# Column units of a split-precision trunk: products in the order hi, hi, lo, lo instead of hi, lo, hi, lo

## The chip, the cores and the metric

The kernel runs on one core of a Trainium2 chip. Times are device microseconds of one execution; the time before is the median of three runs. A profiled execution shows every instruction of each engine: TensorE (PE, with its weight loads as PEld), VectorE (DVE), ScalarE (ACT), GpSimd (POOL) and SyncE (SP), which issues the weight transfers.

## The reference

Two layers of a streaming encoder over 256 tokens of width 2048, all in float32. Each layer normalises, projects, runs eight retention heads and eight blocks of a gated linear recurrence, joins both by an output projection, and ends with a SwiGLU feed-forward part of width 5632:

```python
for l in range(DEPTH):
    h = _rmsnorm(x, norm1_g[l])
    p = (h @ w_in[l]).astype(f32)
    q, k, v, g, xb, yb = jnp.split(p, [R, 2 * R, 3 * R, 4 * R, 4 * R + L], axis=-1)
    ...
    mix = jnp.concatenate([o_ret, o_lru], axis=-1).astype(x.dtype)
    x = x + mix @ w_out[l]
    h = _rmsnorm(x, norm2_g[l])
    x = x + (jax.nn.silu(h @ ffn_w_gate[l]) * (h @ ffn_w_up[l])) @ ffn_w_down[l]
return _rmsnorm(x, final_g)
```

## The kernel before

Activations lie transposed, features on the 128 partitions and the 256 tokens along the row. Every product with a weight matrix is made of float32r products (a reduced float32 that TensorE takes in one pass) of split operands: a high part, which is the value rounded to float32r, and a low part, which is the rest. High by high, high by low and low by high are added up; low by low is left out.

The work is a list of **units**, one for each 128 output features (`layer_units`, line 463). In each layer these are 8 units for v, 40 column units of w_in (with the heads' and the recurrences' work between them), 16 of w_out, and then, for each of three thirds of the feed-forward width (15, 15 and 14 blocks of 128), gate and up units in turn and 16 units of w_down. A unit's weights, up to 128 x 2048, come in one transfer three units ahead (`load`), and are split two units ahead by `split` (line 560) in two halves: ScalarE writes the high half `whi` (line 568), VectorE the low half `wlo` (line 569). Both have three buffers, so ScalarE's next writing waits for TensorE's last reading of a high buffer.

A **column unit** (`column_unit`, line 182) has one PSUM bank `acc_ps` of 512 columns. It goes over its tiles k (16, or 15 and 14 in w_down) in blocks of four; the instructions of heads and recurrences are put between blocks by a counter of ticks. Each tile makes two products. The first takes the tile's high weights against the operand's high and low parts side by side, 512 columns (line 196). The second takes the low weights against the operand's high part, 256 columns, and adds to the upper half of the bank (line 198). Each product has its own load of 128 x 128 weights. At the end ScalarE and VectorE (`joined_halves`, or `residual`) add the two halves.

The v units (lines 441 to 443) have it the other way round: the operand is loaded as weights and 512 columns of weights stream, three products for each tile and half of the tokens (high by high, high by low, low by high). Small products in plain float32 (lines 141 to 331) serve the norms, heads and gates: sums over partitions (141), spreading a row (157), and the heads' transposes (289), which read the normalised halves `on` that VectorE makes at line 275 from a power on GpSimd (line 268).

The program's order within an engine is the order of the code, moved a little by the tile scheduler.

Of the kernel before, what the change touches and what calls it, by code (L numbers as in the profile page):

```python
# [16 lines left out]
P = 128  # L17
T = 256
# [62 lines left out]
def trunk(ctx: ExitStack, tc, a, out):  # L81
# [12 lines left out]
    V, S, G, PE = nc.vector, nc.scalar, nc.gpsimd, nc.tensor  # L94
# [87 lines left out]
    def column_unit(src, n_k, operand, done, begin=None, order=None):  # L182

        u = Unit(src, n_k * P, [], begin=begin)
        order = order or list(range(n_k))

        def block(i):
            ks = order[i : i + 4]

            def run():  # L190
                if i == 0:
                    u.ps = big_ps.tile([P, 512], F32, tag="big", name="acc_ps")
                for k in ks:
                    w = slice(k * P, (k + 1) * P)
                    x2 = operand(k)
                    PE.matmul(u.ps, lhsT=u.hi[:, w], rhs=x2.rearrange("p a t -> p (a t)"),  # L196
                              start=k == order[0], stop=False)
                    PE.matmul(u.ps[:, T : 2 * T], lhsT=u.lo[:, w], rhs=x2[:, 0, :],  # L198
                              start=False, stop=k == order[-1])
            return run  # L200

        u.blocks += [block(i) for i in range(0, n_k, 4)]
        u.done = lambda: done(u.ps)
        return u
# [542 lines left out]
```

## Time and profile before

| | |
|---|---|
| median of 3 runs | 2271.38 us (2269.16 to 2271.72) |
| profiled execution, its own time | 2267.88 us |
| its span | 2266.1 us |
| TensorE | 2249.2 us busy, 99% of the span, 12760 products |
| weight loads | 1955.5 us, 86% |
| VectorE | 1514.8 us, 67% |
| ScalarE | 1127.0 us, 50% |
| GpSimd | 59.8 us, 3% |
| transfers | 422.92 MB, mean 187 GB/s |

The profile has a row for every instruction with its start and, for products, an end that is modelled. A product's record begins before the previous one's ends, so that durations of products add up to more than the time. Rows of the timeline give starts to 0.01 us; longer means come from counts in a stretch. The row of a load names the product that will use the weights.

### The profile page before, as it was taken

To read this page: it belongs to the slowest core of one execution; us is meant where nothing else is said; L and a number is where in the kernel's file an instruction comes from. 1 tells how busy PE (TensorE), PEld (TensorE's weight loads), DVE (VectorE), ACT (ScalarE), POOL (GpSimd) and SP (SyncE) were. 2 spreads that over 40 slices of the span, in tenths; PEclk is the share of its full clock that TensorE was granted. 3 is DMA by queue.
4 is the path that set the end of the run, shared out by engine and by line. 5 is a ranking of instruction groups with operands and counts; after the bars stand their busy time and mean duration, and the time that the engine had idled before them with its cause. 6 is when DMAs were issued, how large, how long until landed. Compare 5 with 4: busy or idle time off the path is not lost.

```text
span 2266.1 us, 31764 instructions
## 1 busy us (share of the span) xinstructions
PE 2249.2 (99%) x12760; PEld 1955.5 (86%) x12760; DVE 1514.8 (67%) x2405; ACT 1127.0 (50%) x1648; POOL 59.8 (3%) x97
## 2 busy tenths in 40 slices
PE   9999999999999999999999999999999999999997
PEld 7888888888888888888888888888888888888886
DVE  6888876666566665666748889766665566566665
ACT  6667544544344443444546665454443444334453
POOL 0010100000000000000000101000000000000000
PEclk9999999999999999999999999999999999999998
DMA  7555455555555555554555554555555555555553
GB/s 286 180 183 179 173 193 188 184 190 190 188 195 186 189 187 190 186 187 173 197 194 180 179 190 166 186 184 188 193 186 189 190 187 183 181 195 188 192 181 109
DMA packets 63141, 422.92 MB, mean 187 GB/s; under 512 B 7313, under 2 KB 7953, under 8 KB 24593
## 3 DMA queue, kind: packets, MB, share of 16 engines
q1 hardware_dynamic: 60912, 414.60, 52.2%
q0 software_dynamic: 1792, 5.24, 0.8%
q8 instruction: 100, 1.64, 0.3%
q10 hardware_dynamic: 288, 1.05, 0.1%
q14 instruction: 49, 0.39, 0.0%
HBM read 418.77 MB, written 2.10 MB: 186 GB/s over the span
## 4 chain that ended last, share of the span: by engine, by line
PE 97%; DVE 1%; issue 0%; DMA 0%; POOL 0%; ACT 0%; SPq 0%; DVEq 0%; POOLq 0%
PE acc_ps L196 61%; PE acc_ps L198 31%; PE v_ps L442 1%; PE v_ps L443 1%; PE v_ps L441 1%; PE sm_ps L331 1%; DVE wlo L569 0%; PE sm_ps L240 0%; DMA raw<-in_w_v_dram 0%; PE sm_ps L157 0%; DVE op L130 0%; PE sm_ps L289 0%; PE sm_ps L241 0%; PE sm_ps L255 0%; PE sm_ps L256 0%
## 5 line engine op out<-in xcount | busy, mean ns | idle before, releaser
L196 PE MATMUL acc_ps<-op,whi 128*128 128x512 f32 x6016 | 2117.0, 397 | 0.0
L198 PE MATMUL acc_ps<-op,wlo 128*128 128x256 f32 x6016 | 1681.1, 279 | 0.0
L196 PEld LDWEIGHTS acc_ps<-op,whi 128*128 128x128 f32 x6016 | 1129.1, 188 | 268.3 <-DVE op L127 1.7
L569 DVE TENSOR_TENSOR wlo<-raw,whi 128x1024 fp32r<-128x1024 f32 (+3 forms) x808 | 948.8, 1189 | 376.1 <-ACT whi L568 368.6
L568 ACT ACTIVATE whi<-raw 128x1024 fp32r<-128x1024 f32 (+3 forms) x808 | 817.1, 1029 | 665.0 <-PE acc_ps L196 587.3
L198 PEld LDWEIGHTS acc_ps<-op,wlo 128*128 128x128 f32 x6016 | 1134.2, 189 | 0.7
L406 DVE TENSOR_TENSOR x<-acc_ps,x 128x256 f32<-128x256 f32 x128 | 54.3, 424 | 216.6 <-PE acc_ps L198 216.6
L126 ACT ACTIVATE op<-mix 128x256 fp32r<-128x256 f32 x104 | 43.1, 416 | 172.3 <-DVE mix L510 163.7
L505 ACT ACTIVATE sg<-z 128x256 f32<-128x256 f32 x88 | 36.8, 418 | 161.2 <-DVE z L504 161.2
L179 DVE TENSOR_TENSOR z<-acc_ps,low 128x256 f32<-128x256 f32 x256 | 106.9, 418 | 0.0
L178 ACT ACTIVATE low<-acc_ps 128x256 f32<-128x256 f32 x256 | 93.7, 366 | 0.0
L127 DVE TENSOR_TENSOR op<-mix,op 128x256 fp32r<-128x256 f32 x104 | 43.9, 424 | 42.6 <-ACT op L126 42.6
L509 DVE TENSOR_TENSOR sg<-sg,rs 128x256 f32<-128x256 f32 x88 | 37.4, 425 | 42.6 <-ACT sg L505 42.6
L407 DVE TENSOR_TENSOR x<-acc_ps,x 128x256 f32<-128x256 f32 x128 | 54.4, 425 | 4.3
L150 POOL TENSOR_TENSOR rc<-rc,mhalf 128x2 f32<-128x2 f32 x7 | 5.8, 824 | 1727.9 <-DVE rc L149 1727.9
L442 PE MATMUL v_ps<-wlo,op 128*128 128x512 f32 x128 | 50.2, 392 | 1.2 <-DVE wlo L569 1.2
L441 PE MATMUL v_ps<-whi,op 128*128 128x512 f32 x128 | 49.9, 395 | 1.3 <-ACT op L129 1.3
L443 PE MATMUL v_ps<-whi,op 128*128 128x512 f32 x128 | 50.2, 392 | 0.0
L504 DVE TENSOR_TENSOR z<-z,rs 128x256 f32<-128x256 f32 x88 | 36.9, 419 | 0.0
L510 DVE TENSOR_TENSOR mix<-z,sg 128x256 f32<-128x256 f32 x88 | 36.9, 419 | 0.0
L129 ACT ACTIVATE op<-x,par 128x256 fp32r<-128x256 f32 x64 | 31.2, 496 | 1.1 <-DMA par<-in_par_dram 1.1
L173 DVE TENSOR_TENSOR acc<-acc,sq 128x256 f32<-128x256 f32 x73 | 30.6, 419 | 1.0 <-ACT sq L172 1.0
(116 smaller groups left out, 699.4 us busy)
## 6 DMA issues: line engine op xcount, KB each, us to landing
raw<-in_w_gate_dram SPq DMA_DIRECT2D x88, 1024.0 KB, 4.8
raw<-in_w_up_dram SPq DMA_DIRECT2D x88, 1024.0 KB, 4.8
raw<-in_w_in_dram SPq DMA_DIRECT2D x80, 1024.0 KB, 4.8
raw<-in_w_down_dram SPq DMA_DIRECT2D x64, 960.0 KB, 4.7
raw<-in_w_out_dram SPq DMA_DIRECT2D x32, 1024.0 KB, 4.8
raw<-in_w_down_dram SPq DMA_DIRECT2D x32, 896.0 KB, 4.6
raw<-in_w_v_dram SPq DMA_DIRECT2D x12, 1024.0 KB, 4.8
raw<-in_w_v_dram SPq DMA_DIRECT2D x16, 256.0 KB, 6.0
```

The lines of the kernel that those rows point to most:

```text
L127: V.tensor_tensor(out=t[:, 1, :], in0=x_ap, in1=t[:, 0, :].bitcast(F32), op=ALU.subtract)
L178: S.activation(out=low, in_=ps[:, T : 2 * T], func=AF.Copy)
L179: V.tensor_tensor(out=z, in0=ps[:, 0:T], in1=low, op=ALU.add)
L196: PE.matmul(u.ps, lhsT=u.hi[:, w], rhs=x2.rearrange("p a t -> p (a t)"), start=k == order[0], stop=False)
L198: PE.matmul(u.ps[:, T : 2 * T], lhsT=u.lo[:, w], rhs=x2[:, 0, :], start=False, stop=k == order[-1])
L406: V.tensor_tensor(out=X[:, k, :], in0=ps[:, T : 2 * T], in1=X[:, k, :], op=ALU.add)
L407: V.tensor_tensor(out=X[:, k, :], in0=ps[:, 0:T], in1=X[:, k, :], op=ALU.add)
L441: PE.matmul(ps, lhsT=x2[:, 0, t], rhs=u.hi[:, w], start=k == 0, stop=False)
L442: PE.matmul(ps, lhsT=x2[:, 0, t], rhs=u.lo[:, w], start=False, stop=False)
L443: PE.matmul(ps, lhsT=x2[:, 1, t], rhs=u.hi[:, w], start=False, stop=k == KD - 1)
L568: S.activation(out=u.hi[:, w], in_=u.raw[:, w], func=AF.Copy)
L569: V.tensor_tensor(out=u.lo[:, w], in0=u.raw[:, w], in1=u.hi[:, w].bitcast(F32), op=ALU.subtract)
```

## The change

Within each block of four tiles, the loop goes over pairs of tiles: both high products of the pair, then both low products. In a block of three the last tile stands alone (high, low). Sums are the same, in another order.

```diff
             def run():
                 if i == 0:
                     u.ps = big_ps.tile([P, 512], F32, tag="big", name="acc_ps")
-                for k in ks:
-                    w = slice(k * P, (k + 1) * P)
-                    x2 = operand(k)
-                    PE.matmul(u.ps, lhsT=u.hi[:, w], rhs=x2.rearrange("p a t -> p (a t)"),
-                              start=k == order[0], stop=False)
-                    PE.matmul(u.ps[:, T : 2 * T], lhsT=u.lo[:, w], rhs=x2[:, 0, :],
-                              start=False, stop=k == order[-1])
+                for pr in (ks[:2], ks[2:]):
+                    for k in pr:
+                        PE.matmul(u.ps, lhsT=u.hi[:, k * P : (k + 1) * P],
+                                  rhs=operand(k).rearrange("p a t -> p (a t)"), start=k == order[0], stop=False)
+                    for k in pr:
+                        PE.matmul(u.ps[:, T : 2 * T], lhsT=u.lo[:, k * P : (k + 1) * P], rhs=operand(k)[:, 0, :],
+                                  start=False, stop=k == order[-1])
             return run
```

TensorE, inside a column unit of w_in in layer 0, before (`op` is an operand's pair of parts, `whi` and `wlo` the unit's weights; the numbers tell buffers apart):

```order
L196 MATMUL acc_ps_887<-op_169,whi_774 128x512
L198 MATMUL acc_ps_887<-op_169,wlo_775 128x256
L196 MATMUL acc_ps_887<-op_182,whi_774 128x512
L198 MATMUL acc_ps_887<-op_182,wlo_775 128x256
L196 MATMUL acc_ps_887<-op_193,whi_774 128x512
L198 MATMUL acc_ps_887<-op_193,wlo_775 128x256
L196 MATMUL acc_ps_887<-op_206,whi_774 128x512
L198 MATMUL acc_ps_887<-op_206,wlo_775 128x256
```

The same four tiles after the change:

```order
L195 MATMUL acc_ps_887<-op_169,whi_774 128x512
L195 MATMUL acc_ps_887<-op_182,whi_774 128x512
L198 MATMUL acc_ps_887<-op_169,wlo_775 128x256
L198 MATMUL acc_ps_887<-op_182,wlo_775 128x256
L195 MATMUL acc_ps_887<-op_193,whi_774 128x512
L195 MATMUL acc_ps_887<-op_206,whi_774 128x512
L198 MATMUL acc_ps_887<-op_193,wlo_775 128x256
L198 MATMUL acc_ps_887<-op_206,wlo_775 128x256
```

The second tile's high product went ahead of the first tile's low one; high products are line 195 now.

TensorE, around the transposes of a late head in layer 0 (`on` is what they read, `sm_ps` what they write), before:

```order
L196 MATMUL acc_ps_2845<-op_169,whi_2684 128x512
L198 MATMUL acc_ps_2845<-op_169,wlo_2685 128x256
L196 MATMUL acc_ps_2845<-op_182,whi_2684 128x512
L289 MATMUL sm_ps_2854<-ident_85,on_2819 128x128
L198 MATMUL acc_ps_2845<-op_182,wlo_2685 128x256
L196 MATMUL acc_ps_2845<-op_193,whi_2684 128x512
L289 MATMUL sm_ps_2854<-ident_85,on_2819 128x128
L198 MATMUL acc_ps_2845<-op_193,wlo_2685 128x256
```

And after:

```order
L195 MATMUL acc_ps_2845<-op_169,whi_2684 128x512
L289 MATMUL sm_ps_2854<-ident_85,on_2819 128x128
L195 MATMUL acc_ps_2845<-op_182,whi_2684 128x512
L198 MATMUL acc_ps_2845<-op_169,wlo_2685 128x256
L198 MATMUL acc_ps_2845<-op_182,wlo_2685 128x256
L289 MATMUL sm_ps_2854<-ident_85,on_2819 128x128
L195 MATMUL acc_ps_2845<-op_193,whi_2684 128x512
```

The first transpose has two products fewer ahead of it, the second one fewer; it is the same in layer 1.

VectorE, at the same place (`on` are the two normalised halves, line 127 the low part of another operand), as a piece of the difference:

```order
 L569 TENSOR_TENSOR wlo_2768<-raw_2585,whi_2767 128x1024
+L275 TENSOR_SCALAR on_2819<-sm_ps_2750,mv_2786,ve_2791 128x128
 L127 TENSOR_TENSOR op_2804<-mix_2802,op_2804 128x256
-L275 TENSOR_SCALAR on_2819<-sm_ps_2750,mv_2786,ve_2791 128x128 x2
+L275 TENSOR_SCALAR on_2819<-sm_ps_2750,mv_2786,ve_2791 128x128
 L179 TENSOR_TENSOR z_2831<-acc_ps_2771,low_2830 128x256
```

The operand's subtraction stands between the two halves now, in layer 0 alone. Two more places differ on VectorE (a weight half ahead of one head's scores, and in the last w_down units of layer 0 the sum of squares between two weight halves) and two on ScalarE (a weight half between two operand copies); GpSimd and SyncE are as before.

## Rows read from the trace of the kernel before

**Rows 1.** The page: busy time by engine, and the chain by engine and line.

```profile
PE 2249.2 (99%) x12760; PEld 1955.5 (86%) x12760; DVE 1514.8 (67%) x2405; ACT 1127.0 (50%) x1648; POOL 59.8 (3%) x97
...
PE 97%; DVE 1%; issue 0%; DMA 0%; POOL 0%; ACT 0%; SPq 0%; DVEq 0%; POOLq 0%
PE acc_ps L196 61%; PE acc_ps L198 31%; PE v_ps L442 1%; PE v_ps L443 1%; PE v_ps L441 1%; PE sm_ps L331 1%; DVE wlo L569 0%; PE sm_ps L240 0%; DMA raw<-in_w_v_dram 0%; PE sm_ps L157 0%; DVE op L130 0%; PE sm_ps L289 0%; PE sm_ps L241 0%; PE sm_ps L255 0%; PE sm_ps L256 0%
```

**Rows 2.** The page's groups: line, tiles, count; busy us, mean ns; idle before.

```profile
L196 PE MATMUL acc_ps<-op,whi 128*128 128x512 f32 x6016 | 2117.0, 397 | 0.0
L198 PE MATMUL acc_ps<-op,wlo 128*128 128x256 f32 x6016 | 1681.1, 279 | 0.0
...
L173 DVE TENSOR_TENSOR acc<-acc,sq 128x256 f32<-128x256 f32 x73 | 30.6, 419 | 1.0 <-ACT sq L172 1.0
```

**Rows 3.** Timeline in w_down, layer 0: start us, duration us, instruction.

```profile
599.74 0.39 PE L196 MATMUL acc_ps<-op,whi 128*128 128x512 f32 x1
599.97 0.28 PE L198 MATMUL acc_ps<-op,wlo 128*128 128x256 f32 x1
599.97 0.19 PEld L196 LDWEIGHTS acc_ps<-op,whi 128*128 128x128 f32 x1
600.08 0.39 PE L196 MATMUL acc_ps<-op,whi 128*128 128x512 f32 x1
...
600.78 0.39 PE L196 MATMUL acc_ps<-op,whi 128*128 128x512 f32 x1
```

**Rows 4.** Timeline 300 us later, first and last of four high products.

```profile
899.75 0.40 PE L196 MATMUL acc_ps<-op,whi 128*128 128x512 f32 x1
...
900.81 0.40 PE L196 MATMUL acc_ps<-op,whi 128*128 128x512 f32 x1
```

**Rows 5.** Line 196 by stretch: length, PE (products), PEld (loads), PEclk; sums of five.

```profile
566.00:811.00 245.00, 245.00 (x708) 132.20 (x707) 1.00 0.54 191
...
sum 872.00, PE 872.00 PEld 471.39; mean PE 174.40 PEld 94.28
...
815.00:1054.00 239.00, 239.00 (x677) 127.05 (x677) 1.00 0.53 187
...
sum 729.00, PE 729.00 PEld 387.57; mean PE 145.80 PEld 77.51
```

**Rows 6.** The same view, two pieces of layer 0's projection, all of layer 1's.

```profile
99.50:117.50 18.00, 18.00 (x52) 9.58 (x51) 1.00 0.53 178
146.50:155.50 9.00, 9.00 (x27) 4.88 (x26) 1.00 0.54 194
1177.00:1430.00 253.00, 236.46 (x661) 123.92 (x660) 1.00 0.52 183
```

**Rows 7.** Timeline in the v units, the first and last of four products.

```profile
1150.03 0.39 PE L442 MATMUL v_ps<-wlo,op 128*128 128x512 f32 x1
...
1150.71 0.39 PE L442 MATMUL v_ps<-wlo,op 128*128 128x512 f32 x1
```

**Rows 8.** Timeline at 43.8 us: eight sums over partitions, merged, with their loads.

```profile
43.81 1.08 PEld L141 LDWEIGHTS sm_ps<-ones,sq 128*128 128x128 f32 x8
...
44.04 0.95 PE L141 MATMUL sm_ps<-ones,sq 128*128 128x1 f32 x8
44.82 0.19 PEld L441 LDWEIGHTS v_ps<-whi,op 128*128 128x128 f32 x1
```

**Rows 9.** Timeline at the last head's transposes in layer 0.

```profile
276.37 0.39 PE L196 MATMUL acc_ps<-op,whi 128*128 128x512 f32 x1
276.95 0.73 DVE L275 TENSOR_SCALAR on<-sm_ps,mv,ve 128x128 f32<-128x128 f32 x2 [0.62 <-POOL ve L268]
...
277.50 0.30 PE L289 MATMUL sm_ps<-ident,on 128*128 128x128 f32 x1 [0.74 <-DVE on L275]
...
277.99 0.27 PE L289 MATMUL sm_ps<-ident,on 128*128 128x128 f32 x1
```

**Rows 10.** Who waited for whom: us in total, times, longest us.

```profile
ACT whi L568 <- PE acc_ps L196: 587.3, 332, 4.0
...
PEld acc_ps L196 <- DVE op L127: 1.7, 6, 0.3
```

## The prediction

> **What bounds the kernel now.** Begin with the busy times and the chain of waits [rows 1]. TensorE is busy 99% of the span, and 97% of the chain that ended last lies on it: 61% on line 196 (the high parts), 31% on line 198 (the low parts). VectorE (67%), ScalarE (50%) and the transfers are cover; the time is set by how closely the 6016 pairs of products follow each other.
>
> The durations of the matmul records don't tell that: 397 and 279 ns [rows 2] overlap, since the next product starts before the record of the last one ends. Go by starts. In the timeline of a w_down stretch [rows 3] a high product starts at 599.74, its low product at 599.97, the next high one at 600.08; three pairs take 1.04 us. The load for that next high product starts at 599.97, together with the low product: each load runs under the product ahead of its own. At the granted 2.4 GHz (PEclk 1.00 in all stretches of [rows 5]) 512 columns take 213.3 ns and 256 take 106.7, 320 together; the spacing is some 26 ns above that.
>
> In another stretch the same instructions stand further apart [rows 4]: 899.75 to 900.81 is 1.06 us for three pairs. Busy time by stretch tells how long each spacing lasts [rows 5]: divide a stretch's length by its loads of line 196, one for each pair. Close: 245 us / 707 = 346.5 ns. Wide: 239 / 677 = 353.0 ns. Five long stretches are close (from 399, 566, 1520, 1941 and 2180 us on), 872 us together, so 2517 pairs; five are wide (from 309, 815, 1058, 1430 and 1686 on), 729 us, so 2065 pairs. The same piece of the program (w_down of the first third, then gate and up of the second) runs close from 566 in layer 0 and wide from 1686 in layer 1: the spacing belongs to no kind of unit. It changes where something interrupts the stream, and then stays. The input projections (660 loads in that of layer 1, as many in the other) are interrupted often and hold both spacings: 18 us / 51 = 352.9 in one piece and 9 / 26 = 346.2 in another [rows 6].
>
> **The change part by part.** Nothing is added or taken away: the same 12,032 products and loads, with the same columns. Two high products now follow each other, then two low ones; of 6016 tiles only 64 (the 15th of w_down's units with 15 tiles) stay high, low. Three effects:
>
> 1. *The spacing.* Before, every load of low weights ran under a high product and every load of high weights under a low one. Now, of four loads, two still run under high and two under low products; new is that high follows high and low follows low. High after high has a near row: in the v units products of 512 columns, each with a load of its own, start 0.68 us apart for three (1150.03 to 1150.71), 226.7 ns each [rows 7]. In the close spacing high to low takes 230 ns and low to high the rest, 116.5 [rows 3], so v's is 3.3 ns less. Low after low has no row. Its lower bound is the 106.7 ns of its columns. Its upper bound is the spacing of loads that nothing covers: eight loads with products of one column took 1.08 us, the last of them 0.19, so (1.08 - 0.19) / 7 = 127 ns each [rows 8]. I take 116.5, the nearest row, since there, too, a load must end under 256 columns. For high after high I take the 230 of this kind of unit and keep v's 226.7 for the range. Two tiles then cost 2 x 346.5 ns, the close spacing, and as the one uniform sequence that the trace has (v) keeps its spacing, I take it to last. Gain: 2065 pairs x 6.5 ns = 13.4 us, and in the projections half of some 1320 x 6.5 ns = 4.3 us (between 0 and 8.6). Together -17.7 us.
>
> 2. *The order around the transposes.* In each layer TensorE waits once for the last head's normalised halves: it does a high product at 276.37 and then nothing until 277.50, when the first transpose follows the half that VectorE began at 276.95; the second is at 277.99 [rows 9]. The new order has two products fewer ahead of the first transpose, 0.23 + 0.12 us that now stand behind the wait: +0.35 us a layer. VectorE puts an operand's subtraction (0.42 us) between the two halves in layer 0; three products instead of two now lie between the transposes and hide it, or else it is 0.4 us more. Two small spreads move up by one product of 0.12 us a layer, at a wait as well. Sum +0.9 us, between 0 and 1.3. ScalarE's moved copies and the moved sums in the last w_down third of layer 0 I cost at 0: two further units are already split. Without that cover a moved sum would be 0.42 us [rows 2] a unit, on 15 units 6 us.
>
> 3. *Releases and first uses.* A unit's last high product ends one low product (0.12 us) earlier, and ScalarE, which waited for it 332 times, 587.3 us in all [rows 10], may overwrite the buffer earlier. That wait isn't on the chain: worth 0. The last product of a unit stays a low one, so residuals and gates begin as before. In the second tile of a pair an operand is read 0.12 us earlier; TensorE's six waits for operands were 1.7 us [rows 10], so this is 0.7 us at most, and I take 0.
>
> Sum: -17.7 + 0.9 = -16.8 us on the profiled 2267.9 us, which gives 2251.1. The median of the runs shown is 2271.4, 3.5 us above the profiled one, so 2254.6 there.
>
> **Rivals.**
>
> *No change of the mean: both spacings remain.* For: what is counted under what is the same in both orders (two loads under long, two under short products for two tiles), and the spacings change after interruptions, which the change leaves in place. Some stretches then swap spacings; one of 700 pairs is worth 700 x 6.5 = 4.6 us. Time: 2272, within 9. Against: another rhythm need not have the old two spacings. The Trainium skill (TensorE: Matmul & The Clock Gate, "LDWEIGHTS (loading the stationary operand)") has a rule on this side: a load takes its columns over 1.2 GHz, 107 ns for 128, which is as long as 256 columns stream; by that every load just fits under either product, in either order, and the sum would be 0. The trace agrees only in part: low to high takes some 10 ns more than that.
>
> *Slower: two short products in a row can't cover two loads.* The place is the second low product of each pair of tiles. Its load begins only when the first low product does, and the next one's when it begins itself; before, a long product, in which a late stream catches up, came behind each short cover. If the gap there is the 127 ns of [rows 8] in place of 116.5, that is 10.5 ns x 3008 = +32 us on the close spacing, 2286. If the new rhythm settles in the wide spacing everywhere, it is 2517 x 6.5 = 16.4, 4.3 and 0.9 us above before: 2293. It decides from 17.7 us / 3008 = 5.9 ns per two tiles on; there the gain is eaten up. For: low to high is the gap in which a load has least cover. Against: 116.5 ns shows that a load does end under 256 columns.
>
> *Faster still.* With v's 226.7 ns from high to high it is 3.3 x 3008 = 10 us less, 2244.6, and with high to low at 226.7 as well 2235. Against: 3 ns may be only where a record begins.
>
> **How the numbers follow.** About 0.2% (4.5 us) is what a measurement of this kernel can tell from no change. The close spacing throughout, or better, has a chance of 0.42; both spacings 0.26 (0.07 faster, 0.13 the same, 0.06 slower); slower by the loads or the wide spacing 0.32. So faster 0.49, same 0.13, slower 0.38. The forecast is 2254.6, with a range of its own of 2242 to 2262. As cases of both signs count, the range is 2238 to 2296: it leaves out v's spacing in both gaps, and a 127 ns gap on top of the wide spacing.
>
> **What would show it.** In the timeline: high to high and high to low 0.23 us, low to low and low to high 0.12, two tiles in 0.693 us, and this in all ten long stretches, none at 0.706. Wrong would be a gap of 0.127 or more from low to low, or stretches that still differ. The transposes of the last head should wait some 0.35 us longer, and TensorE keep its 97% of the chain.

## The result and the profile after

The changed kernel takes 2257.81 us (median of 4 runs, 2257.48 to 2258.28) against 2271.35 us before (4 runs, 2269.16 to 2271.72): a ratio of 0.9938, with a 95% interval of 0.9926 to 0.9951, 13.5 us less. In a later comparison of 6 with 11 runs it was 2258.33 against 2272.65, 0.9930 (0.9917 to 0.9942). The profiled execution took 2257.48 us, 10.4 less than that of before.

The page after, busy times, chain and the two groups of products, to be held against [rows 1, 2]:

```profile
PE 2239.1 (99%) x12760; PEld 1949.4 (86%) x12760; DVE 1512.5 (67%) x2405; ACT 1127.1 (50%) x1648; POOL 59.8 (3%) x97
...
PE 97%; DVE 1%; issue 0%; DMA 0%; POOL 0%; ACT 0%; SPq 0%; DVEq 0%; POOLq 0%
...
L195 PE MATMUL acc_ps<-op,whi 128*128 128x512 f32 x6016 | 1899.8, 397 | 0.0
...
L198 PE MATMUL acc_ps<-op,wlo 128*128 128x256 f32 x6016 | 1188.6, 278 | 0.0
```

Nothing changed its part: TensorE has 97% of the chain, VectorE and ScalarE do as much as before. The busy sums of lines 195 and 198 fell by 217 and 493 us only because records of the same line that overlap now count once; the mean records, 397 and 278 ns, are those of before. So go by starts. The timeline after (`x2` is two instructions, the start is the first one's), at the place of [rows 3]:

```profile
600.02 0.39 PE L198 MATMUL acc_ps<-op,wlo 128*128 128x256 f32 x2
...
600.25 0.63 PE L195 MATMUL acc_ps<-op,whi 128*128 128x512 f32 x2
...
600.71 0.40 PE L198 MATMUL acc_ps<-op,wlo 128*128 128x256 f32 x2
...
600.94 0.40 PE L195 MATMUL acc_ps<-op,whi 128*128 128x512 f32 x1
```

Two low products take 0.23 us (600.02 to 600.25), two high ones 0.46 (to 600.71), together some 0.695 for two tiles. Line 195 by stretch (length; products; loads), to be held against [rows 5]:

```profile
566.00:808.00 242.00, 218.60 (x696) 106.30 (x695) 1.00 0.54 189
815.00:1045.00 230.00, 207.82 (x661) 100.98 (x660) 1.00 0.54 188
...
1679.00:1925.00 246.00, 222.25 (x707) 107.93 (x705) 1.00 0.54 190
```

242 / 695 = 348.2, 230 / 660 = 348.5 and 246 / 705 = 348.9 ns a tile (a load counted too many or too few is 0.5 ns). Before, the stretch from 815 was wide (353.0), that from 566 close (346.5) and that from 1686 wide. All three have one spacing now, 1.7 to 2 ns above the close one and nearly 5 below the wide one.

Where the time came from can be read off four markers, the sums over partitions at the end of w_out and of the feed-forward part in each layer. Before:

```profile
395.65 0.61 PE L141 MATMUL sm_ps<-ones,acc 128*128 128x1 f32 x4
1135.58 0.61 PE L141 MATMUL sm_ps<-ones,acc 128*128 128x1 f32 x4
1516.86 0.61 PE L141 MATMUL sm_ps<-ones,acc 128*128 128x1 f32 x4
2251.04 0.50 PE L529 MATMUL sm_ps<-ones,acc 128*128 128x1 f32 x4
```

After:

```profile
392.70 0.50 PE L141 MATMUL sm_ps<-ones,acc 128*128 128x1 f32 x4
1129.96 0.54 PE L141 MATMUL sm_ps<-ones,acc 128*128 128x1 f32 x4
1508.53 0.50 PE L141 MATMUL sm_ps<-ones,acc 128*128 128x1 f32 x4
2241.20 0.50 PE L529 MATMUL sm_ps<-ones,acc 128*128 128x1 f32 x4
```

The lead grows to 2.95, 5.62, 8.33 and 9.84 us: 2.95 in layer 0's projections, heads and w_out, 2.67 in its feed-forward part, 2.71 and 1.51 in layer 1. In the feed-forward parts, stretches that had been close cost a little more and the wide ones much less.

The wait at the last head's transposes after the change ([rows 9] show it before):

```profile
274.10 0.39 PE L195 MATMUL acc_ps<-op,whi 128*128 128x512 f32 x1
...
274.97 0.41 DVE L275 TENSOR_SCALAR on<-sm_ps,mv,ve 128x128 f32<-128x128 f32 x1 [0.92 <-POOL ve L268]
...
275.53 0.30 PE L289 MATMUL sm_ps<-ident,on 128*128 128x128 f32 x1 [1.04 <-DVE on L275]
...
276.14 0.28 PE L289 MATMUL sm_ps<-ident,on 128*128 128x128 f32 x1
```

From the start of the last high product to the first transpose it was 1.13 us (276.37 to 277.50) and is now 1.43: 0.30 more, at the place that the new order gave. In layer 1 the lead falls by 0.30 us at the same place.

### The profile page after: what moved, and what is told of

The parts are those of the page before. It is cut to its first block, busy times and chain, and to the rows that moved or that the text cites. A ratio compares the mean times of both kernels' runs of the same rounds, so it can differ in the third digit from the quotient of the medians.

```text
span 2255.7 us, 31764 instructions
## 1 busy us (share of the span) xinstructions
PE 2239.1 (99%) x12760; PEld 1949.4 (86%) x12760; DVE 1512.5 (67%) x2405; ACT 1127.1 (50%) x1648; POOL 59.8 (3%) x97
## 4 chain that ended last, share of the span: by engine, by line
PE 97%; DVE 1%; issue 0%; DMA 0%; POOL 0%; ACT 0%; SPq 0%; DVEq 0%; POOLq 0%
PE acc_ps L195 62%; PE acc_ps L198 31%; PE v_ps L442 1%; PE v_ps L443 1%; PE v_ps L441 1%; PE sm_ps L331 1%; DVE wlo L569 0%; PE sm_ps L240 0%; DMA raw<-in_w_v_dram 0%; DVE op L130 0%; PE sm_ps L289 0%; PE sm_ps L157 0%; PE sm_ps L241 0%; PE sm_ps L256 0%; PE sm_ps L255 0%
## 5 line engine op out<-in xcount | busy, mean ns | idle before, releaser
L195 PE MATMUL acc_ps<-op,whi 128*128 128x512 f32 x6016 | 1899.8, 397 | 0.0
L198 PE MATMUL acc_ps<-op,wlo 128*128 128x256 f32 x6016 | 1188.6, 278 | 0.0
L195 PEld LDWEIGHTS acc_ps<-op,whi 128*128 128x128 f32 x6016 | 920.4, 189 | 4.8 <-DVE op L127 0.7
L179 DVE TENSOR_TENSOR z<-acc_ps,low 128x256 f32<-128x256 f32 x256 | 106.7, 417 | 0.0
```

The source lines that it names most:

```text
L179: V.tensor_tensor(out=z, in0=ps[:, 0:T], in1=low, op=ALU.add)
L195: PE.matmul(u.ps, lhsT=u.hi[:, k * P : (k + 1) * P], rhs=operand(k).rearrange("p a t -> p (a t)"), start=k == order[0], stop=False)
L198: PE.matmul(u.ps[:, T : 2 * T], lhsT=u.lo[:, k * P : (k + 1) * P], rhs=operand(k)[:, 0, :], start=False, stop=k == order[-1])
```

## The experiments

**Is the spacing chosen by the place, or by chance?** First, the kernel before once more, without an edit (`before_2`).

> The kernel before, unchanged, profiled once more. If each interruption leaves the old order in one of two spacings by a chance of timing, other stretches than in the first profile are close and wide, and the time differs by the pairs that changed (6.67 ns each) within some 2263 to 2282. If the place decides, the same five stretches are close (from 399, 566, 1520, 1941 and 2180 us on).

It took 2275.07 us, 7.2 more than its first profile. Line 196 by stretch:

```profile
399.00:561.00 162.00, 162.00 (x460) 86.17 (x459) 1.00 0.51 181
570.00:815.00 245.00, 245.00 (x694) 130.25 (x694) 1.00 0.53 185
824.00:1062.00 238.00, 238.00 (x675) 126.63 (x674) 1.00 0.53 186
...
1695.00:1944.00 249.00, 249.00 (x706) 132.47 (x705) 1.00 0.53 187
1949.00:2183.00 234.00, 234.00 (x677) 126.22 (x676) 1.00 0.54 190
```

162 / 459 = 352.9 and 245 / 694 = 353.0: both stretches were close in the first profile (468 loads in the first, and 707 in 245 us). The same program, on the same instructions, was wide there. 1175 pairs by 6.5 ns are 7.6 us, near the difference of the two executions. So the place alone doesn't decide, and stretches that come out close or wide can explain why runs of the kernel before differ from each other: beside the groups of experiments below they lay between 2260.42 and 2281.71 us. But it isn't plain chance either. The other eight long stretches had the spacing of the first profile; three of them are shown (353.1, 353.2 and 346.2 ns). In the four profiles of the old order in these widths (`before`, `before_2`, and below `kick_before` and `lolow`) the stretches that begin at 309, 815, 1430 and 1686 in the first one are wide each time, and that from 1941 is close each time; the other five differ. What makes the choice stays open.

Then 37 small interruptions, one extra product of one column each, in either kernel (`kick_before`, `kick_after`):

```diff
     for n, u in enumerate(units):
+        if n >= 64 and n % 9 == 4:
+            PE.matmul(small()[:, 0:1], lhsT=ones, rhs=ones[:, 0:1], start=True, stop=True)
         if u.begin:
```

> The kernel before, with one extra product of a single column (float32, into a PSUM tile that nothing reads) ahead of every ninth unit from the 64th on, 37 in all. Theory 'two rhythms' (the old order has two spacings, 346.5 and 353.0 ns a tile, and an interruption decides which one follows): the long stretches break up, some pieces between two extra products run at 346.5 and some at 353.0; time 2271 plus 37 x 0.1 to 0.3 us, so 2275 to 2282, with a change of the mix worth up to 13 us either way. Rival 'place' (the spacing belongs to the place in the program, by its buffers or transfers): each piece keeps the spacing it had, close from 566 on and wide from 815 on.

> The changed kernel with the same 37 extra products. Theory 'one rhythm' (hi, hi, lo, lo has a single spacing, 348.3 ns a tile, to which every interruption returns): all pieces at 348.3, time 2257.8 plus 37 x 0.1 to 0.3 us, so 2262 to 2269. Rival 'chance' (the new order has two spacings as well, and the interruptions happened to leave it in the closer one): some pieces near 353, up to 2285.

Measured: 2282.98 us (2277.98 to 2286.37) and 2266.60 us (2266.23 to 2267.18). Line 196 between the extra products, old order:

```profile
412.00:459.00 47.00, 47.00 (x136) 25.32 (x136) 1.00 0.51 179
462.00:509.00 47.00, 47.00 (x137) 25.35 (x136) 1.00 0.50 181
...
610.00:656.00 46.00, 46.00 (x131) 24.43 (x130) 1.00 0.53 182
659.00:707.00 48.00, 48.00 (x137) 25.55 (x136) 1.00 0.51 177
...
761.00:809.00 48.00, 48.00 (x137) 25.52 (x136) 1.00 0.51 174
...
909.00:957.00 48.00, 48.00 (x137) 25.51 (x136) 1.00 0.51 177
```

136 loads need 47 us in the first pieces and 48 us in later ones, 346 and 353 ns; the wide pieces at 610 and 761 lie where the first profile was close. But the extra products didn't do this. 31 of the 37 stand outside the projections, in long stretches (that at 459.7 us between the first two pieces, that at 656.5 between the next two), and behind each of the 31 the spacing is the one ahead of it. From w_out on, in all four profiles of the old order, the spacing changes only at the start of a feed-forward part and near the end of the first unit of each w_down. There TensorE waits for an operand that has just been made (in units of 14 tiles the scheduler has also put two high products in a row there). In the first profile, at 564.26:

```profile
564.26 0.19 PEld L196 LDWEIGHTS acc_ps<-op,whi 128*128 128x128 f32 x1 [0.33 <-DVE op L127]
```

Line 195 in the new order:

```profile
409.00:456.00 47.00, 42.40 (x136) 20.41 (x135) 1.00 0.51 179
...
656.00:703.00 47.00, 42.40 (x136) 20.57 (x136) 1.00 0.52 181
...
903.00:949.00 46.00, 41.47 (x134) 20.09 (x132) 1.00 0.52 183
```

135 or 136 loads in 47 us and 132 in 46, and runs within 0.95 us, against 8.4 us in the old order. 'One rhythm' holds, 'chance' falls. As the extra products don't move the old order either, they say little by themselves; what bears it out is that the new order has the same spacing behind each wait for an operand, in this profile and in those of the changed kernel. The old order was wide in more places here than in the first profile, which can account for part of its 11.5 us over the kernel before beside it (2271.45).

The changed kernel in more runs, without an edit (`after_2`):

> The changed kernel, unchanged, in more runs. If its rhythm doesn't depend on what an execution leaves it in, all runs lie within 2256.5 to 2259.5 while those of the kernel before beside it spread over 10 us or more, and its profile has 348.3 ns a tile in all stretches. If the first runs were luck, some lie 4 us or more away. Against the version with whole units grouped (2257.14) it should be 0.5 to 1 us slower, if that difference is real.

2258.33 us (2257.55 to 2258.59); those of the kernel before beside it spread from 2270.71 to 2278.00, 7.3 us rather than 10. The spacing in its profile is 348.2 again (695 loads from 566 to 808), and near 348 in all ten long stretches.

**Is it the change of width that costs?** Groups of four and of eight tiles (`g4`, `g8`):

```diff
-                for pr in (ks[:2], ks[2:]):
+                for pr in (ks,):
```

> The changed kernel with groups of four: hi, hi, hi, hi, lo, lo, lo, lo in each block. Theory 'rhythm' (what matters is whether the pattern locks, the loads under long and short products being as many as before): 346.7 to 353.3 ns a tile, time 2247 to 2290, no gain that grows with the length of the group. Rival 'change of width' (the time above the streams of 320 ns is paid where the width changes): high after high nears the 226.7 ns of the v units and low after low 113, so 341.6 ns a tile or less, 40 us below the changed kernel, 2218.

For eight, blocks one and two (three and four) of a unit share their eight tiles: six high products, then two high and eight low.

> Groups of eight: of every eight tiles all high products, then all low ones. Rhythm: as with four, 2247 to 2290, and the gaps inside a run of high products still above 226.7 ns on average or the gaps inside a run of low ones at 120 (256 columns and the same 13.3 ns that a product of 512 columns has above its stream in the v units). Change of width: 340 ns a tile, 2208; high after high 226.7, low after low 113.

Measured: 2269.90 us (2268.95 to 2270.64) and 2264.94 us (2264.10 to 2265.31), both slower than pairs. High products by stretch, with four (line 195) and with eight (line 194):

```profile
570.00:815.00 245.00, 191.04 (x700) 119.25 (x700) 1.00 0.54 189
```

```profile
567.00:812.00 245.00, 175.83 (x702) 126.14 (x703) 1.00 0.54 189
```

350.0 ns and 348.5 to 349. Longer runs didn't come near the 341.6 or 340 ns of 'change of width'. Half the change (`g2mix`):

```diff
-                for pr in (ks[:2], ks[2:]):
+                for pr in (ks[:2], ks[2:3], ks[3:]):
```

> Blocks of four tiles as hi, hi, lo, lo, hi, lo, hi, lo: half of the change. Theory 'one rhythm for each pattern': a single spacing between 346.7 (13.3 ns for each product above its stream, the least seen) and 353.3, little spread between runs, time 2248 to 2288. Rival 'mean of the two': 348.3 in the grouped half and 346.5 or 353 in the alternating half, times that spread by some 5 us between runs.

2275.14 us (2274.93 to 2275.52): one rhythm, with the least spread of all, and a bad one. Line 195:

```profile
570.00:815.00 245.00, 232.44 (x698) 119.07 (x698) 1.00 0.53 188
```

351.0 ns, more than equal shares of the grouped order (348.2) and of the alternating one (350, the mean of close and wide) would make. With an alternating half that is always wide (353.0) equal shares would make 350.6, so the time alone doesn't tell a spacing of the pattern's own from a wide half that keeps. What is shown is that this pattern, too, varies little from run to run.

Whole units (`g16`): all high products of a unit, then all low ones, in blocks of 6 high, 6 high, 4 high and 4 low, 12 low (5384 of the 6016 tiles; w_out, the first gate unit and the first unit of each w_down stay in pairs):

```diff
+                if whole:
+                    j = i // 4
+                    steps = [((0, 6), (0, 0)), ((6, 12), (0, 0)), ((12, n_k), (0, 4)), ((0, 0), (4, n_k))][j]
...
+                for k in (range(*steps[0]) if whole else []):
...
+                for k in (range(*steps[1]) if whole else []):
```

> The changed kernel, but in w_in, gate, up and w_down units (not in w_out, nor in the first gate and first w_down units) all high products of a unit go ahead of all low ones. By 'two widths' with the 20 ns that a change from the runs of low to the runs of high took with eight, now once in 16 tiles: 346.7 + 20 / 16 = 347.9 ns a tile against 348.3, 2 us below the changed kernel, 2255 to 2258, if no operand is waited for longer; with later waits up to 2262. If the cost grows with the run (four: 350.3, eight: 349.2) rather than standing for a change: 348 to 350, 2258 to 2268.

2257.14 us (2256.45 to 2257.63; ratio to before 0.9947, 0.9930 to 0.9965). Three windows of its timeline, from 600, 601.9 and 604.2 us on, in a w_down unit of 15 tiles, give the number of products of each run that a window still holds, and the start of the first of them (line 200 high, 203 low):

```profile
600.14 3.59 PE L200 MATMUL acc_ps<-op,whi 128*128 128x512 f32 x15
603.57 1.96 PE L203 MATMUL acc_ps<-op,wlo 128*128 128x256 f32 x15
605.36 0.40 PE L200 MATMUL acc_ps<-op,whi 128*128 128x512 f32 x1
```

```profile
601.53 2.20 PE L200 MATMUL acc_ps<-op,whi 128*128 128x512 f32 x9
```

```profile
603.92 1.60 PE L203 MATMUL acc_ps<-op,wlo 128*128 128x256 f32 x12
```

The last nine high products take 603.57 - 601.53 = 2.04 us, 226.7 ns each, the value of the v units [rows 7]; the last twelve low ones 1.44 us, 120.0 each. So in a long run a product costs 13.3 ns more than its columns at 2.4 GHz (213.3 and 106.7 ns), at both widths. After the change from low to high the first six high products take 1.39 us, 231.7 each, 30 ns more in all; the first three low ones 0.35 us, 10 ns less than three of 120. A unit therefore pays 20 ns, and 5.22 us / 15 = 348.0 a tile. Two products at these long-run costs, 226.7 + 120.0 = 346.7, are the close spacing of the old order. No order tried here settled below this floor: the close stretches had nothing to gain, and only the wide ones could be won back.

**Is the load too long for its cover?** Low products of 128 columns (`lo128`; the low weights are left out for the last 128 tokens):

```diff
-                    PE.matmul(u.ps[:, T : 2 * T], lhsT=u.lo[:, w], rhs=x2[:, 0, :],
+                    PE.matmul(u.ps[:, T : T + 128], lhsT=u.lo[:, w], rhs=x2[:, 0, 0:128],
```

> The kernel before, hi and lo in turn, with low products of 128 columns in place of 256 (the low weights are left out for the last 128 tokens). Theory 'load' (under a low product the load of the next weights is what ends last, some 112 to 120 ns): low to high stays at 112 to 120 ns and a tile at 340 to 353, time 2230 to 2272 although 53 ns of streaming a tile are gone. Rival 'stream' (a product costs its columns and 13.3 ns, as 226.7 for 512 in the v units and 120 for 256 inside the runs of eight): low to high 67 ns, a tile 293, time about 1920.

2229.41 us (two runs): 53 ns less streaming a tile bring 43 us against the kernel before beside it (2272.41), not 320. (In the profiled run the granted clock fell to 1.2 GHz in four short pieces of the projections, 17 us together; the stretch read below has 2.4 GHz.) The timeline and line 196 by stretch:

```profile
600.14 0.22 PE L198 MATMUL acc_ps<-op,wlo 128*128 128x128 f32 x1
600.15 0.19 PEld L196 LDWEIGHTS acc_ps<-op,whi 128*128 128x128 f32 x1
600.20 0.44 PE L196 MATMUL acc_ps<-op,whi 128*128 128x512 f32 x1
600.25 0.19 PEld L198 LDWEIGHTS acc_ps<-op,wlo 128*128 128x128 f32 x1
600.48 0.22 PE L198 MATMUL acc_ps<-op,wlo 128*128 128x128 f32 x1
...
570.00:780.00 210.00, 210.00 (x619) 115.92 (x618) 1.00 0.55 195
```

A tile is 210 us / 618 = 339.8 ns, and 339.8 - 226.7 leaves 113 ns from low to high, far more than the low product's columns: the load. My forecast of the gap was wrong in its form. The high product's record begins 0.06 us after the low one, 0.05 after its own load began. In the other timelines a load starts together with the product ahead of its own; here the load of the next low weights starts at 600.25, so that is where the high product's stream began, 0.11 after 600.14. No run shows less than 226.7 ns for a high product, so a load takes 113 ns at most, 7 less than the 120 of a low product. It may be shorter: from the load of the high weights to the next load (600.15 to 600.25) it is 107.7 ns on the mean of 500 tiles from 600 to 770 us, and what is left of the tile, 232.3, is then a high product with some 6 ns of the extra that the wide spacing has as well. The Trainium skill (TensorE: Matmul & The Clock Gate, "LDWEIGHTS (loading the stationary operand)") gives a load its columns over 1.2 GHz, by which 128 columns would take 107 ns, an estimate that the run doesn't contradict. At 113 or less it fits under every gap of the other orders, of which the shortest, from low to low, are 113 to 115 ns; it sets the time here at 128 columns, and not at 320 or 512.

The other side, low products of 320 columns (`lo320`):

```diff
-                    PE.matmul(u.ps[:, T : 2 * T], lhsT=u.lo[:, w], rhs=x2[:, 0, :],
+                    PE.matmul(u.ps[:, 0:320], lhsT=u.lo[:, w], rhs=x2.rearrange("p a t -> p (a t)")[:, 0:320],
```

> The kernel before with low products of 320 columns (they go to the lower half of the bank and take in 64 tokens of the operand's low part; more is added up than before, nothing is left out). Theory 'load' (the old order has a wide spacing because the load of the high weights barely fits under 256 columns): with 26.7 ns more cover there is one spacing, the streams of 346.7 and twice 13.3 ns, 373.3 a tile in every stretch, time 2271 + 22 x 6.016 = 2403, and less spread between runs. Rival 'rhythm of two widths' (any alternation of two widths has a wide spacing): some stretches above 376, time up to 2440.

2444.98 us. Line 196:

```profile
430.00:600.00 170.00, 170.00 (x448) 84.04 (x447) 1.00 0.49 171
700.00:900.00 200.00, 200.00 (x528) 99.01 (x527) 1.00 0.48 171
```

380 ns a tile in both, 6.7 above the floor of 373.3: with more cover for the load the wide rhythm, 6.7 ns above the floor, came everywhere. 'Load' falls as the cause of the wide spacing. With 512 columns, both widths alike (`lo512`; low by low is added):

```diff
-                    PE.matmul(u.ps[:, T : 2 * T], lhsT=u.lo[:, w], rhs=x2[:, 0, :],
+                    PE.matmul(u.ps, lhsT=u.lo[:, w], rhs=x2.rearrange("p a t -> p (a t)"),
```

> The kernel before with low products of 512 columns, the same width as the high ones (the low part of the operand by the low weights is added, which the kernel before leaves out). Theory 'two widths' (what a tile takes above 13.3 ns a product is paid where the width of the products alternates): one spacing, 2 x 226.7 = 453.3 ns a tile as in the v units, time about 2271 + 102 x 6.016 = 2885, no wide stretch. Rival 'order of weights' (the extra comes from going back and forth between the two weight buffers): 460 ns a tile or two spacings, 2925.

2888.00 us, and

```profile
750.00:1000.00 250.00, 214.49 (x553) 103.50 (x552) 1.00 0.42 146
```

250 us / 552 = 452.9 ns, the 453.3 of two equal products, though the weight buffers alternate as before. With one width the extra is gone.

**Has PSUM a part in it?** Low products to the lower half of the bank (`lolow`):

```diff
-                    PE.matmul(u.ps[:, T : 2 * T], lhsT=u.lo[:, w], rhs=x2[:, 0, :],
+                    PE.matmul(u.ps[:, 0:T], lhsT=u.lo[:, w], rhs=x2[:, 0, :],
```

> The kernel before with the low products added to the lower half of the bank in place of the upper one; the halves are added up in the end, so the result is the same sum. Theory 'load': PSUM has no part in it, two spacings of 346.5 and 353 and times between 2264 and 2282 as before. Rival 'PSUM' (a product is held up because the one ahead has just written the same columns): another spacing, equal in all stretches.

2271.13 us (2266.17 to 2276.77), with both spacings:

```profile
399.00:561.00 162.00, 162.00 (x468) 87.64 (x468) 1.00 0.53 187
...
815.00:1050.00 235.00, 234.96 (x665) 124.81 (x666) 1.00 0.53 185
```

346.2 and 352.9 ns. Which columns are added to makes no difference that shows.

## Why the prediction was right, and where its sizes were off

*The bound.* TensorE's spacing of products decided nearly all of the change, and its two values were read rightly from the starts; the second profile of before shows them at other places. The prediction's "It changes where something interrupts the stream" was too wide: waits for an operand can change it, while 31 extra products in the long stretches never did.

*The spacing, one for the new order.* Right in kind: one spacing everywhere. It was neither the close one nor the wide one, and no case of the forecast had that. The step "I take 116.5" and "the 230 of this kind of unit" gave two tiles 2 x 346.5 ns, and they take 0.696 us, 2 x 348.2. Of the two, the low gaps were right (0.23 us for two, 115 each), and the high ones too small (0.46 us, near 233 each). The row of whole units has the same size: there, too, the first high products after a change of width stand further apart than 226.7 ns, and a pair has no others. Why that is so no run shows. The v units, a long run of one width, were the wrong row to infer steadiness at the best spacing from. By the terms of the sum: 2065 wide pairs gained 353.0 - 348.2 = 4.8 ns, 9.9 us in place of 13.4; the 2517 close pairs, forecast at 0, lost 1.7 ns, 4.3 us. Starts at the same places in both traces give the shares: w_out and the feed-forward parts of both layers brought 7.0 us in all, the projections 2.9 (1.5 and 1.4; without the loss at the transposes 3.5 us, forecast 4.3), the two ends of the program 0.6.

The profiles differ by 10.4 us where the sum had 16.8, so the sum was 6.4 us too large. That the forecast of the median is only 3.2 us too low is partly luck. It carries over the 3.5 us by which the median before stood above its profile, and that distance came from an execution with many close stretches; after the change it is 0.3 us (2257.81 against 2257.48). For the same reason the medians differ by 13.5 us.

*The order around the transposes.* Forecast +0.35 us a layer, measured +0.30 in each. Releases and first uses showed nothing, as taken.

*The rival 'both spacings remain'* is refuted by the profiles of the changed kernel (`after`, `after_2`) and by `kick_after`: no long stretch of theirs is wide. *The rival 'two short products can't cover two loads'* fails by the timeline after and by `lo128`: low after low stays near 115 ns (120 in a long run), not 127, and a load takes 113 ns at most. The 127 ns of [rows 8] were loads of float32 products in another mix, an upper bound that was too far. *'Faster still'* fell with the 233 ns of high after high.

*What stays open.* Why an alternation of 512 and 256 columns has two steady spacings, of 512 and 320 only the one 6.7 ns above its floor, and groups of 2, 4 and 8 tiles 348.2, 350.0 and 349, isn't settled. The runs speak against the load's length (`lo320`), the PSUM columns (`lolow`) and the change of weight buffer (`lo512`). In `lo512` the extra went with the second width, but how two widths would make it no run shows. Which of the two spacings the old order takes after a wait is open too: the place has a part in it and isn't all. Whether whole units beat pairs is open: 2257.14 against 2257.81 and 2258.33 lie in separate comparisons.

## What to carry to other kernels

When one engine is busy 99% of the span, count instructions by stretch and divide. Two spacings of the same instructions in the same kernel, with times that differ from run to run, are time to be won that no busy share shows. A pattern of products that returns to one spacing after each wait can beat one whose best spacing is better but isn't kept. Choose the pattern by measuring it: groups of four and eight tiles were slower here than pairs, and whole units only drew level. And an interruption that is put in on purpose shows something only if it can move what it is to test; here the extra products moved neither order.

## What the runs showed that was not expected

A product with a load of its own costs its columns and 13.3 ns in a long run, at 256 as at 512 columns (120.0 and 226.7 ns). The Trainium skill (TensorE: Matmul & The Clock Gate, "Back-to-back issue gap") gives 2.5 ns above the columns for a single product by itself, by which 512 columns would take 216 ns, an estimate, and 131 ns a product for a stream of products of 512 columns with their loads. Long runs of products of 512 columns, each with its own load, took 226.7 ns here, above both figures, and the measurement decides. A product's record can begin 0.06 us after the last one's start, before its stream does (`lo128`); the start of the next load tells when the stream began. And the kernel before, unchanged, ran anywhere from 2260.42 to 2281.71 us; in the two executions that were profiled, the difference was two long stretches that were close in one and wide in the other.
